# A decoder block on one core: the first token tile takes its norm weight per channel on the transposed rows, its loads go out on two queues, and constant products stand ahead of the first ones

## The chip, the core and the metric

The kernel runs on one core of one Trainium2 chip. TensorE (PE) multiplies; VectorE (DVE), ScalarE (ACT) and GpSimd (POOL) do the rest; SyncE (SP) issues most transfers from memory. The metric is the device time of one execution in microseconds (us). The kernel before took 1122.25 us (median of three runs, 1120.26 to 1123.79).

## The reference

One layer of a hybrid block over 512 tokens of width 1024, in float32:

```python
u = rmsnorm(h, norm_mix_pre_w[layer])          # x * rsqrt(mean(x*x) + eps) * w
proj = u @ w_in[layer]
q, k, v, z, xbc, dt_raw, gate_logits = jnp.split(proj, offsets, axis=-1)
# dilated attention on q, k, v; a Mamba-2 mixer on z, xbc, dt_raw; both projected,
# mixed by sigmoid gates, projected again, normed and added to h; then a squared-ReLU MLP
```

Only the first line and the `v` and `dt_raw` columns of the second one are touched here. The norm weight `w` has one value per channel.

## The kernel before

Every float32 product is made of three products of rounded halves: a matrix is split into a high part (`wh`, `uh`: a rounding copy on ACT) and a low part (`wl`, `ul`: the remainder, by a subtraction on DVE or POOL), and `three` issues high by high, low by high and high by low. Weights come as units of 1 MB through a two-deep pool (`ws` staging, `wh`, `wl`).

The start, from L264 on, makes `u` transposed (channels on partitions) for four tiles of 128 tokens. For a tile `i`, `square_u` squares the rows with a running sum (ACT, L300 and L303), adds eps (DVE, L301 and L304) and takes the power -1/2 on POOL (L305). `norm_u` (L309) multiplies the rows by this factor and by `row0`, the norm weight broadcast to all partitions. `transpose_u` (L212) turns eight blocks of 128 by 128 on PE into two PSUM banks `ut`. `split_u` (L321 and L322) makes `uh` and `ul` of a bank at a time, four channel blocks in one instruction.

Between these steps stand the splits of the first weight chunk, `split_v1` (L326, L327), in four pieces of two channel blocks. The three value chunks are then computed in the order 1, 0, 2 (`V_ORDER`), for four token tiles each, with the squares, norms and transposes of the tiles 1 to 3 put between the products of the tile before (`V_STEPS`). A product chunk is called `psv` in rows, chunk 1's being the first four. Chunk 0 also holds the `dt_raw` columns; its weights are `wh0` and `wl0` (L331, L332, the second half of `wl0` on POOL). The weights of chunk 2 come through the pool (L108) and are split by L90 and L93.

Two things set the order on an engine. Instructions marked with `pin` keep the order in which they are written; others are put by the scheduler. Not pinned are the splits of chunk 2, the exponential of `a_log` on ACT (L409, `rows`), and the evacuations `vtok`. Each engine then runs its list in order. Transfers on SP each take one of eight completion semaphores in turn, and a transfer waits until the one eight places before it has landed.

In the rows, `wh_v` and `wl_v` name the parts of any value chunk; the line tells which (L326 and L327 are chunk 1, L331 and L332 chunk 0, L90 and L93 chunk 2).

Of the kernel before, what the change touches and what calls it, by code (L numbers as in the profile page):

```python
# [11 lines left out]
F32 = mybir.dt.float32  # L12
# [6 lines left out]
P = 128  # L19
# [23 lines left out]
SSM_FILL = (2, 7, 4, 3, 9, 5, 6)  # L43
SSM_LAST = (3, 8, 4, 3, 9, 8, 8)

V_ORDER = tuple((d, i) for d in (1, 0, 2) for i in range(NT))
# [31 lines left out]
def hybrid_block(ctx: ExitStack, tc: tile.TileContext, a: dict):  # L78
# [126 lines left out]
    def pin(ins):  # L205
        return tc.keep_in_program_order(ins)
# [53 lines left out]
    with tc.tile_pool(name="start", bufs=1, reuse_waits="tile") as st:  # L260
# [9 lines left out]
        def load_x(i):  # L270
            for cs in (slice(0, T), slice(T, D)) if i == 0 else (slice(0, D),):
                sp.dma_start(xt[:, i, cs], a["x"][0, i * P : (i + 1) * P, cs])

        def load_row(cs):
            sp.dma_start(row0[:, cs], a["norm_mix_pre_w"][:, cs].broadcast_to([P, T]))
# [3 lines left out]
                         for n, dt in (("ws", F32), ("wh", F32R), ("wl", F32R))]  # L279
        load_row(slice(0, T))  # L280
        for k in range(0, KD, 2):
            sp.dma_start(v3(ws1, KD)[:, k : k + 2, :], w_in[:, k : k + 2, OFF_V + UC : OFF_V + 2 * UC])
            if k == 0:
                load_row(slice(T, D))
            if k == KD - 2:
                load_x(1)
        for i in range(2, NT):
# [8 lines left out]
        def square_u(i):  # L296
            un = uns[i] = st.tile([P, D], F32, name=f"un{i}", tag="un", bufs=2)
            if i == 0:
                for n, cs in enumerate((slice(0, T), slice(T, D))):
                    pin(act.activation(un[:, cs], xt[:, i, cs], AF.Square, scale=RD, accum_out=sq0[:, n : n + 1]))  # L300
                pin(dve.tensor_scalar(rs[:, i : i + 1], sq0[:, 0:1], sq0[:, 1:2], EPS, ALU.add, ALU.add))  # L301
            else:
                pin(act.activation(un, xt[:, i, :], AF.Square, scale=RD, accum_out=ssq[:, i : i + 1]))  # L303
                pin(dve.tensor_scalar(rs[:, i : i + 1], ssq[:, i : i + 1], EPS, None, ALU.add))  # L304
            pin(pool.tensor_tensor(rs[:, i : i + 1], rs[:, i : i + 1], mhalf, op=ALU.pow))  # L305

        def norm_u(i):
            for cs in (slice(0, T), slice(T, D)):
                pin(dve.scalar_tensor_tensor(uns[i][:, cs], xt[:, i, cs], rs[:, i : i + 1], row0[:, cs],  # L309
                                             op0=ALU.mult, op1=ALU.mult))  # L310
# [7 lines left out]
        def split_u(i, b):  # L318
            p3 = pts.pop((i, b)).rearrange("p (k t) -> p k t", k=4)
            hi = uh[:, 4 * b : 4 * b + 4, i * P : (i + 1) * P]  # L320
            pin(act.activation(hi, p3, AF.Copy))  # L321
            pin(dve.tensor_tensor(ul[:, 4 * b : 4 * b + 4, i * P : (i + 1) * P], p3, hi.bitcast(F32), op=ALU.subtract))  # L322

        def split_v1(k, eng=dve):
            ks = slice(k * UC, (k + 2) * UC)
            pin(act.activation(wh1[:, ks], ws1[:, ks], AF.Copy))  # L326
            pin(eng.tensor_tensor(wl1[:, ks], ws1[:, ks], wh1[:, ks].bitcast(F32), op=ALU.subtract))  # L327

        def split_v0(k, eng=dve):
            ks = slice(k, k + 4)  # L330
            pin(act.activation(wh0[:, ks, :], ws0[:, ks, :], AF.Copy))  # L331
            pin(eng.tensor_tensor(wl0[:, ks, :], ws0[:, ks, :], wh0[:, ks, :].bitcast(F32), op=ALU.subtract))  # L332

        square_u(0)
        norm_u(0)
        split_v1(0)
        transpose_u(0, 0)
        transpose_u(0, 1)
        split_v1(2, pool)
        split_u(0, 0)  # L340
        split_v1(4)
        split_u(0, 1)
        split_v1(6)
# [743 lines left out]
```

## Time and profile before

| | |
|---|---|
| median of 3 runs | 1122.25 us |
| the profiled execution | 1122.04 us, span 1120.3 us |
| PE busy in the span | 1094.8 us (98%) |
| DVE, ACT, POOL busy | 670.7, 482.2, 63.4 us |
| chain that ended last | PE 89%, DVE 7%, DMA 2% |
| TensorE's mean granted clock | 0.997 of full |

The span runs from the first to the last instruction of the execution; 1.7 us of the profiled execution lie around it. The page says that a busy PE is not PE at its peak, since matmul ends are modelled: the distance between the starts of two neighbours tells more than a duration. What the change touches lies in the first 45 us.

### The profile page before, as it was taken

The numbers are of one execution on the slowest core, as the hardware profiler recorded it, in microseconds if no ns is written. First come the engines' busy times: TensorE is split into PE (matmuls) and PEld (weight loads), VectorE is DVE, ScalarE is ACT, GpSimd is POOL, SyncE is SP. The second block draws the span as 40 slices with busy tenths as digits, with TensorE's granted clock in tenths as the row PEclk, the third lists the DMA queues.
The fourth block names the chain that finished last, engine by engine and source line by source line (L and its number), as shares of the span: only waits on it lengthen the run. The fifth ranks groups of instructions, "written<-read, shape, count | busy, mean of one in ns | idle before, by whom it ended". The sixth has DMA issues, their size and how long they took to land.

```text
span 1120.3 us, 13600 instructions
## 1 busy us (share of the span) xinstructions
PE 1094.8 (98%) x5501; PEld 909.5 (81%) x5501; DVE 670.7 (60%) x986; ACT 482.2 (43%) x803; POOL 63.4 (6%) x71
## 2 busy tenths in 40 slices
PE   6999999999999999999999999999999999999997
PEld 6988877778888787878787878889888888888886
DVE  5657665347786869696969685855433234333324
ACT  6256665463556363637272623443322233232321
POOL 2203222000000000000000000000000000000000
PEclk9999999999999999999999999999999999999999
DMA  8232212332333232332323222450332324223212
GB/s 274 77 114 77 69 45 66 104 94 77 112 97 129 76 113 80 108 100 89 113 75 113 76 76 77 187 188 1 113 113 75 113 86 159 102 86 114 75 38 75
DMA packets 86463, 110.86 MB, mean 99 GB/s; under 512 B 4080, under 2 KB 74224, under 8 KB 85376
## 3 DMA queue, kind: packets, MB, share of 16 engines
q1 hardware_dynamic: 85072, 101.01, 28.2%
q0 software_dynamic: 1328, 8.98, 2.1%
q8 instruction: 43, 0.70, 0.3%
q14 instruction: 20, 0.16, 0.0%
HBM read 107.81 MB, written 2.16 MB: 98 GB/s over the span
## 4 chain that ended last, share of the span: by engine, by line
PE 89%; DVE 7%; DMA 2%; issue 1%; ACT 1%; SPq 0%; POOL 0%; POOLq 0%; DVEq 0%; ACTq 0%
PE psu L209 16%; PE psd L209 15%; PE psx L209 8%; PE psbc L209 8%; PE psz L209 8%; PE pssp L209 5%; PE psga L209 4%; PE psgs L209 4%; PE psq L209 3%; PE psk L209 3%; PE psap L209 3%; PE psv L209 3%; PE pq L209 1%; PE po L209 1%; PE pt L212 1%; DVE acc L679 1%
## 5 line engine op out<-in xcount | busy, mean ns | idle before, releaser
L209 PE MATMUL psu<-fh,wh_up 128*128 128x512 f32 (+1 forms) x288 | 105.4, 366 | 0.0
L209 PE MATMUL psu<-fl,wh_up 128*128 128x512 f32 (+1 forms) x288 | 105.2, 365 | 0.0
L209 PE MATMUL psu<-fh,wl_up 128*128 128x512 f32 (+1 forms) x288 | 105.2, 365 | 0.0
L209 PE MATMUL psd<-wl_dn,hh 128*128 128x512 f32 x240 | 93.4, 389 | 0.0
L209 PE MATMUL psd<-wh_dn,hl 128*128 128x512 f32 x240 | 93.4, 389 | 0.0
L209 PE MATMUL psd<-wh_dn,hh 128*128 128x512 f32 x240 | 93.4, 389 | 0.0
L93 DVE TENSOR_TENSOR wl_up<-ws_up,wh_up 128x2048 fp32r<-128x2048 f32 x16 | 36.7, 2292 | 77.6 <-ACT wh_up L90 77.5
L93 DVE TENSOR_TENSOR hl<-hidden,hh 128x512 fp32r<-128x512 f32 x32 | 21.9, 693 | 77.3 <-ACT hh L90 77.2
L90 ACT ACTIVATE hh<-hidden 128x512 fp32r<-128x512 f32 x32 | 20.2, 632 | 103.1 <-PE psd L209 97.6
L209 PEld LDWEIGHTS psu<-fh,wh_up 128*128 128x128 f32 x288 | 54.3, 189 | 8.8
L209 PEld LDWEIGHTS psu<-fh,wl_up 128*128 128x128 f32 x288 | 54.3, 189 | 8.7
L209 PEld LDWEIGHTS psu<-fl,wh_up 128*128 128x128 f32 x288 | 54.3, 189 | 8.7
L90 ACT ACTIVATE wh_up<-ws_up 128x2048 fp32r<-128x2048 f32 x16 | 30.7, 1916 | 61.4 <-PE psu L209 56.1
L209 PEld LDWEIGHTS psd<-wh_dn,hh 128*128 128x128 f32 x240 | 45.0, 188 | 9.5
L209 PEld LDWEIGHTS psd<-wh_dn,hl 128*128 128x128 f32 x240 | 45.0, 188 | 9.4
L209 PEld LDWEIGHTS psd<-wl_dn,hh 128*128 128x128 f32 x240 | 45.0, 188 | 9.3
L209 PE MATMUL psx<-uh,wh_x 128*128 128x512 f32 x128 | 52.4, 410 | 0.0
L209 PE MATMUL psz<-uh,wh_z 128*128 128x512 f32 x128 | 51.1, 399 | 0.0
L209 PE MATMUL pssp<-yth,wh_sp 128*128 128x512 f32 x128 | 51.0, 399 | 0.0
L209 PE MATMUL psbc<-uh,wh_bc 128*128 128x512 f32 x128 | 50.8, 397 | 0.0
L209 PE MATMUL psz<-uh,wl_z 128*128 128x512 f32 x128 | 50.1, 392 | 0.0
L209 PE MATMUL pssp<-yth,wl_sp 128*128 128x512 f32 x128 | 50.1, 392 | 0.0
(271 smaller groups left out, 2792.4 us busy)
## 6 DMA issues: line engine op xcount, KB each, us to landing
ws_up<-in_w_up_dram SPq DMA_DIRECT2D x16, 1024.0 KB, 5.4
ws_dn<-in_w_down_dram SPq DMA_DIRECT2D x15, 1024.0 KB, 5.0
ws_z<-in_w_in_dram SPq DMA_DIRECT2D x8, 1024.0 KB, 5.2
ws_x<-in_w_in_dram SPq DMA_DIRECT2D x8, 1024.0 KB, 5.2
w<-acs_d POOLq DMA_DIRECT2D x8, 1024.0 KB, 5.0
ws_bc<-in_w_in_dram SPq DMA_DIRECT2D x16, 512.0 KB, 4.7
ws_sp<-in_w_ssm_proj_dram SPq DMA_DIRECT2D x8, 1024.0 KB, 4.8
ws_ga<-in_w_in_dram SPq DMA_DIRECT2D x4, 1024.0 KB, 5.3
```

What stands on the lines that cost most here:

```text
L90: ins = act.activation(hi, src, AF.Copy)
L93: (eng or dve).tensor_tensor(lo, src, hi.bitcast(F32), op=ALU.subtract)
L209: tc.keep_in_program_order(pe.matmul(*args, **kw))
L212: tc.keep_in_program_order(pe.transpose(dst, src, ident))
L679: dve.tensor_tensor(acc[o], acc[o], ps, op=ALU.add)
```

## The change

The first token tile is no longer multiplied by the broadcast norm weight. Its rows are only scaled by their own factor; after the transposes channels lie on partitions, and `split_u0` applies the weight as a scale per partition (`ncol`, 8 values per partition) in the same instructions that split, now one channel block at a time: eight on ACT and eight on DVE in place of two and two. The second half of the tile's rows is squared on DVE, by an instruction that multiplies and sums, beside the first half's square on ACT. That second half and `ncol` are loaded from ACT's queue. SP issues the four weight pieces and tile 1's rows before the two halves of `row0`. Eleven products of a constant tile stand at the head of PE's list, into a bank that nothing reads. The third piece of `wl` of chunk 1 moves from POOL to DVE.

```diff
         def load_x(i):
-            for cs in (slice(0, T), slice(T, D)) if i == 0 else (slice(0, D),):
-                sp.dma_start(xt[:, i, cs], a["x"][0, i * P : (i + 1) * P, cs])
+            if i == 0:
+                act.dma_start(xt[:, 0, T:], a["x"][0, 0:P, T:])
+                sp.dma_start(xt[:, 0, :T], a["x"][0, 0:P, :T])
+            else:
+                sp.dma_start(xt[:, i, :], a["x"][0, i * P : (i + 1) * P, :])
...
-        load_row(slice(0, T))
+
+        ncol = st.tile([P, KD], F32, name="ncol")
+        act.dma_start(ncol, a["norm_mix_pre_c"])
         for k in range(0, KD, 2):
             sp.dma_start(v3(ws1, KD)[:, k : k + 2, :], w_in[:, k : k + 2, OFF_V + UC : OFF_V + 2 * UC])
-            if k == 0:
-                load_row(slice(T, D))
-            if k == KD - 2:
-                load_x(1)
+        load_x(1)
+        load_row(slice(0, T))
+        load_row(slice(T, D))
...
-                for n, cs in enumerate((slice(0, T), slice(T, D))):
-                    pin(act.activation(un[:, cs], xt[:, i, cs], AF.Square, scale=RD, accum_out=sq0[:, n : n + 1]))
+                pin(act.activation(un[:, :T], xt[:, i, :T], AF.Square, scale=RD, accum_out=sq0[:, 0:1]))
+                pin(dve.tensor_tensor_reduce(un[:, T:], xt[:, i, T:], xt[:, i, T:], 1.0 / D, 0.0, ALU.mult, ALU.add,
+                                             sq0[:, 1:2]))
...
+                if i == 0:
+                    pin(dve.tensor_scalar(uns[i][:, cs], xt[:, i, cs], rs[:, i : i + 1], None, ALU.mult))
+                    continue
...
+        def split_u0(k):
+            pk = pts[0, k // 4][:, (k % 4) * P : (k % 4 + 1) * P]
+            hi = uh[:, k, 0:P]
+            pin(act.activation(hi, pk, AF.Copy, scale=ncol[:, k : k + 1]))
+            pin(dve.scalar_tensor_tensor(ul[:, k, 0:P], pk, ncol[:, k : k + 1], hi.bitcast(F32), op0=ALU.mult,
+                                         op1=ALU.subtract))
...
+        warm = gbank("warm")
+        for n in range(WARM):
+            mm(warm[:, 0:P], ones, ones, start=True, stop=True)
         square_u(0)
         norm_u(0)
-        split_v1(0)
         transpose_u(0, 0)
         transpose_u(0, 1)
-        split_v1(2, pool)
-        split_u(0, 0)
+        split_u0(0)
+        split_u0(1)
+        split_v1(0)
+        split_u0(2)
+        split_u0(3)
+        split_v1(2)
+        split_u0(4)
+        split_u0(5)
         split_v1(4)
-        split_u(0, 1)
+        split_u0(6)
+        split_u0(7)
         split_v1(6)
         square_u(1)
```

The scheduler's order differs only in the first 45 us. On ACT, the work of the first tile (`uh` out of `ut`, the pieces `wh_v` of chunk 1) stood so before:

```order
L326 ACTIVATE wh_v_108<-ws_v_107 128x512 [waits DMAHW3_49]
L326 ACTIVATE wh_v_108<-ws_v_107 128x512 [waits DMAHW5_49]
L321 ACTIVATE uh<-ut_0_133 128x4x128 [waits PE_49]
L326 ACTIVATE wh_v_108<-ws_v_107 128x512 [waits DMAHW6_49]
L321 ACTIVATE uh<-ut_1_138 128x4x128 [waits PE_49]
L326 ACTIVATE wh_v_108<-ws_v_107 128x512 [waits DMAHW7_49]
```

And now, the first half of the same list (semaphores in brackets; DMAHW ones are a transfer's landing):

```order
L337 ACTIVATE uh<-ut_0_145,ncol 128x128 [waits DMAHW2_49,PE_49]
L337 ACTIVATE uh<-ut_0_145,ncol 128x128 [waits DVE_49]
L343 ACTIVATE wh_v_108<-ws_v_107 128x512 [waits DMAHW3_49]
L337 ACTIVATE uh<-ut_0_145,ncol 128x128 [waits DVE_49] x2
L343 ACTIVATE wh_v_108<-ws_v_107 128x512 [waits DMAHW4_49]
```

Each `uh` but the first of a bank now waits for DVE's `ul` of the block before it.

Further on in ACT's list, the tiles 1 to 3 stood so before (`un` are squares, `rows` the exponential of `a_log`, `vtok` evacuations; `wh_v_101` is chunk 0, `wh_v_314` chunk 2):

```order
L303 ACTIVATE un_187,ssq<-xt 128x1024
L321 ACTIVATE uh<-ut_0_200 128x4x128
L321 ACTIVATE uh<-ut_1_205 128x4x128
L365 ACTIVATE vtok<-psv_0_177 128x256
L303 ACTIVATE un_230,ssq<-xt 128x1024
L321 ACTIVATE uh<-ut_0_240 128x4x128
L409 ACTIVATE rows<-rows 128x32
L321 ACTIVATE uh<-ut_1_245 128x4x128
L365 ACTIVATE vtok<-psv_1_223 128x256
L321 ACTIVATE uh<-ut_0_282 128x4x128
L321 ACTIVATE uh<-ut_1_287 128x4x128
L331 ACTIVATE wh_v_101<-ws_v_100 128x1152 x2
```

And now (`wh_v_340` is chunk 2):

```order
L310 ACTIVATE un_213,ssq<-xt 128x1024
L436 ACTIVATE rows<-rows 128x32
L331 ACTIVATE uh<-ut_0_226 128x4x128
L331 ACTIVATE uh<-ut_1_231 128x4x128
L392 ACTIVATE vtok<-psv_0_203 128x256
L310 ACTIVATE un_256,ssq<-xt 128x1024
L331 ACTIVATE uh<-ut_0_266 128x4x128
L331 ACTIVATE uh<-ut_1_271 128x4x128
L392 ACTIVATE vtok<-psv_1_249 128x256
L92 ACTIVATE wh_v_340<-ws_v_338 128x1024 x2
L331 ACTIVATE uh<-ut_0_308 128x4x128
L331 ACTIVATE uh<-ut_1_313 128x4x128
```

The exponential moved from the middle of tile 2 to ahead of tile 1's split, and chunk 2's high parts from behind chunk 0's to ahead of tile 3's split.

On DVE, the end of the same stretch stood so before (`ul` from `ut_0_282` on is tile 3, `wl_v_102` chunk 0, `wl_v_315` chunk 2):

```order
L309 SCALAR_TENSOR_TENSOR un_230<-xt,rs,row_98 128x512 x2
L322 TENSOR_TENSOR ul<-ut_0_282,uh 128x4x128
L322 TENSOR_TENSOR ul<-ut_1_287,uh 128x4x128
L332 TENSOR_TENSOR wl_v_102<-ws_v_100,wh_v_101 128x1152
L93 TENSOR_TENSOR wl_v_315<-ws_v_312,wh_v_314 128x1024 x2
```

And now:

```order
L319 SCALAR_TENSOR_TENSOR un_256<-xt,rs,row_98 128x512 x2
L95 TENSOR_TENSOR wl_v_341<-ws_v_338,wh_v_340 128x1024 x2
L332 TENSOR_TENSOR ul<-ut_0_308,uh 128x4x128
L332 TENSOR_TENSOR ul<-ut_1_313,uh 128x4x128
L349 TENSOR_TENSOR wl_v_102<-ws_v_100,wh_v_101 128x1152
```

Chunk 2's low parts moved ahead of tile 3's. On POOL, the power for tile 3 moved behind three small multiplications of `cw`, `cb` and `bg`.

## Rows read from the trace of the kernel before

**Rows 1.** Busy time by stretch; PE busy, PEld, DVE, ACT, POOL, PEclk, DMA share, GB/s.
```profile
19.90:52.00 32.10, 32.10 (x260) 32.10 (x259) 20.75 (x39) 11.59 (x21) 10.09 (x8) 1.00 0.45 139
...
200.00:790.00 590.00, 580.23 (x3013) 480.92 (x3012) 429.36 (x626) 281.52 (x480) 17.28 (x24) 1.00 0.31 99
```
**Rows 2.** The chain of waits from 0 to 60 us: start, length, what.
```profile
4.79 7.55 DMA xt<-in_x_dram
...
12.36 1.16 ACT un L303 x2
...
23.70 28.63 PE psv L209 x228
```
**Rows 3.** PE in order of time: start, duration, instruction, idle time before and its releaser.
```profile
7.76 1.12 PE L212 MATMUL ut<-ident,un 128*128 128x128 f32 x4 [7.76 <-DVE un L309]
...
12.51 0.41 PE L209 MATMUL psv<-wh_v,uh 128*128 128x256 f32 x1
12.72 0.41 PE L209 MATMUL psv<-wl_v,uh 128*128 128x256 f32 x1
...
14.27 0.28 PE L209 MATMUL psv<-wl_v,uh 128*128 128x256 f32 x1
14.39 0.28 PE L209 MATMUL psv<-wh_v,ul 128*128 128x256 f32 x1
...
24.98 0.29 PE L209 MATMUL psv<-wh_v,uh 128*128 128x256 f32 x1
```
**Rows 4.** The waits of PE from 200 us on: total, times, longest.
```profile
PE pyo L209 <- DVE prev L759: 9.6, 11, 1.4
```
**Rows 5.** ACT in order of time, same columns as PE's.
```profile
9.59 0.63 ACT L326 ACTIVATE wh_v<-ws_v 128x512 fp32r<-128x512 f32 x1 [1.38 <-DMA ws_v<-in_w_in_dram]
10.13 0.58 ACT L321 ACTIVATE uh<-ut 128x512 fp32r<-128x512 f32 x1
...
15.94 1.19 ACT L321 ACTIVATE uh<-ut 128x512 fp32r<-128x512 f32 x2 [1.08 <-PE ut L212]
...
19.76 0.22 ACT L409 ACTIVATE rows<-rows 128x32 f32<-128x32 f32 x1
...
26.65 2.01 ACT L90 ACTIVATE wh_v<-ws_v 128x1024 fp32r<-128x1024 f32 x2
```
**Rows 6.** DVE in order of time.
```profile
6.96 0.75 DVE L309 SCALAR_TENSOR_TENSOR un<-xt,rs,row 128x512 f32<-128x512 f32 x1 [1.82 <-DMA row<-in_norm_mix_pre_w_dram]
...
14.37 1.41 DVE L309 SCALAR_TENSOR_TENSOR un<-xt,rs,row 128x512 f32<-128x512 f32 x2 [0.67 <-POOL rs L305]
```
**Rows 7.** SP's queue in order of time: start and duration of an issue.
```profile
0.73 0.84 SPq L272 DMA_DIRECT2D xt<-in_x_dram  x2
...
11.27 3.67 SPq L346 DMA_DIRECT2D rows<-in_dt_bias_dram  x1
14.98 0.43 SPq L346 DMA_DIRECT2D rows<-in_a_log_dram  x1
...
20.12 0.38 SPq L108 DMA_DIRECT2D ws_v<-in_w_in_dram  x1
```
**Rows 8.** Transfers issued from 11 to 24 us: size, us from issue to landing.
```profile
ws_v<-in_w_in_dram SPq DMA_DIRECT2D x1, 1024.0 KB, 5.4
...
rows<-in_a_log_dram SPq DMA_DIRECT2D x1, 16.0 KB, 4.4
```
**Rows 9.** Groups by shape on ACT, 0 to 60 us: busy, mean ns, idle before.
```profile
L397 ACT ACTIVATE dt<-dt 128x128 f32<-128x128 f32 x1 | 0.3, 310 | 0.8 <-DVE dt L396 0.8
```
**Rows 10.** Groups by shape on DVE, 0 to 60 us.
```profile
L322 DVE TENSOR_TENSOR ul<-ut,uh 128x512 fp32r<-128x512 f32 x8 | 5.3, 687 | 3.1 <-ACT uh L321 3.1
...
L93 DVE TENSOR_TENSOR wl_q<-ws_q,wh_q 128x1024 fp32r<-128x1024 f32 x2 | 2.3, 1210 | 0.0
L327 DVE TENSOR_TENSOR wl_v<-ws_v,wh_v 128x512 fp32r<-128x512 f32 x3 | 2.1, 711 | 0.0
L404 DVE SCALAR_TENSOR_TENSOR dt<-dt,dt 128x128 f32<-128x128 f32 x7 | 2.0, 292 | 0.2
```

More of the change, by code (lines that the diff above doesn't have):

```diff
@@ L44 @@
 SSM_LAST = (3, 8, 4, 3, 9, 8, 8)
+WARM = 11
 V_ORDER = tuple((d, i) for d in (1, 0, 2) for i in range(NT))
@@ L1072 @@
     data["ssm_norm_w"] = data["ssm_norm_w"][0].reshape(16, P).T
+    data["norm_mix_pre_c"] = data["norm_mix_pre_w"][0].reshape(8, P).T
     data["d_skip"] = _np.repeat(data["d_skip"][0], P // 2).reshape(16, P).T
```

## The prediction

> **What bounds the kernel now.** I read the busy times by stretch first. From 19.9 us to 52 PE is busy all the time, and between 200 and 790 us 580.2 of 590 us [rows 1]; what PE loses at the start is therefore not made up by waiting for something else just after. The chain of waits says the same of the start: up to 12.36 us it waits for the rows of tile 1 to land, goes through their square and norm, and from 23.70 us it is 28.63 us of products without a break [rows 2]. So the question is when PE gets through the last piece of chunk 1, tile 3, whose first product starts at 24.98 us and whose third, the first to read `ul`, comes some 0.24 us later, at 25.22 (the products at 14.27 and 14.39 are 0.12 apart) [rows 3]. Everything behind it keeps its order on every engine, so I take its shift as the kernel's shift.
>
> Then I read ACT and DVE in order of time, since the change alters their lists. ACT runs its list strictly: at 9.59 us it had been idle 1.38 us for a weight piece, and the rounding of the first transposed bank, whose operand PE began at 7.76, had to stand behind it until 10.13 [rows 3, 5]. An instruction that waits for a landing holds all that is listed after it. That decides this change.
>
> **The first tile, earlier.** Before, DVE could start the norm at 6.96 us only because it waited 1.82 us for the broadcast weight [rows 6]; that wait goes, and one of two squares leaves ACT, for some 0.6 us more (the gap between two 128x512 copies there is 0.54 [rows 5]; the form on DVE isn't in the trace: at the cheapest 128x512 form, 0.69, it ends with ACT's square, at twice that the gain is gone). So the norm starts at about 4.6 to 5.2 us, and the transposes at 6.0, having 7.76 before. I cost the eleven constant products at nothing: PE is idle there until 7.76 [rows 3]. Should the transposes have to wait for them, a microsecond is lost in a place that, as follows, no longer decides.
>
> **The first tile, then slower.** Per pair of channel blocks the new lists alternate: `uh` on ACT (0.31), `ul` on DVE (0.29), the next `uh`, which waits for that `ul` (0.31), a weight piece's high part (0.63), its low part on DVE (0.71), and only then the next pair's `ul`, since DVE's list has it behind the low part. In steady state a pair costs the second `uh`, the high part, the low part and the first `ul` of the next pair: 0.31 + 0.63 + 0.71 + 0.29 = 1.94 us [rows 5, 9, 10]. (The 128x128 forms read SBUF there, PSUM here; above, each is bounded by the 0.69 of a whole bank.) If ACT alone decided it would be 2 x 0.31 + 0.63 = 1.25. Four pairs from about 6.7 us on: 14.5 us, or 11.7 at best. ACT's square of tile 1 follows, 1.06 and 0.19 of read-out, then eps, power and norm: before, that took from 12.36 to 14.37 [rows 2, 6], so the norm of tile 1 starts at 16.5 (13.7 at best) against 14.37. The early start is spent.
>
> **The wait for `a_log`.** The exponential now stands ahead of tile 1's `uh`. Its operand was issued at 14.98 us and took 4.4 [rows 7, 8]: 19.4. Before, it ran at 19.76, after tile 1's `uh` of 15.94 [rows 5], and cost nothing. Now tile 1's `uh` cannot start before 19.4 + 0.22 = 19.6. Behind it in ACT's list stand tile 1's second half, an evacuation and the square of tile 3; DVE's `ul`, the norm of tile 2 (behind `ul` in its list) and so tile 2's transposes wait for it. From `uh` to the end of tile 2's products I count: 0.58 + 0.69 until `ul`, 0.69 for the second `ul`, the norm of tile 2 (1.41), four transposes (0.5), half a group of products (1.4), a whole one (2.9) with eight transposes (1.0): 9.2 us, so that tile 3's first product could start at 28.8. That alone is 3.8 us late.
>
> **The wait for chunk 2's weights.** Both ACT and DVE now split chunk 2 ahead of tile 3. These weights were issued at 20.12 us and took 5.4 [rows 7, 8]: 25.5. Then the first high half takes 1.06 (26.6; two took 2.01 [rows 5]), the two low halves 1.21 each [rows 10] (29.0), tile 3's first `ul` 0.69 (29.7). Before, the product that reads it started at 25.22: 4.4 us late. The two waits run beside each other and don't add: the later one, this one, counts. Chunk 0 follows with no further loss: its POOL half ends 2.8 us after its high part, as before, and tile 3's products and half a group of chunk 0 cover it (2.6 + 1.6 us).
>
> **When these transfers land now.** SP's list from the third tile's rows on is the same, and so are the bytes ahead. The 3.67 us issue of `dt_bias` [rows 7] shows that the queue was full then, and the issues behind it came as it drained. The front is relieved by one issue of 0.42 us, now on ACT. I take 0.5 us earlier: 25.0, and tile 3 then 3.9 us late. Bounds: not earlier at all (4.4), or 1.9 earlier, if half of the 3.67 us goes (2.5); if all of it went, chunk 2 would make 0.7 us, but then tile 1 is held by its own norm, 16.5 against 14.37, 2.1 us.
>
> The second queue is the place where the Trainium skill speaks against the change. "DMA: Bandwidth & Descriptors", section "Issuing engines are not separate DMA queues", says that transfers started by different engines share the same 16 DMA engines and that only the issuer's time is saved. By that the halves land 0.4 us earlier at most, as I took above; were the second queue worth both issues of the first rows, 0.84 us [rows 7], tile 3 would be 3.6 us late. No row here has two queues at once.
>
> **The sum.** Gains: none reaches tile 3. Loss: 3.9 us, with a little for a TensorE that is idle or sparsely used until 19 us: before, its 128x256 products were 0.21 us apart at 12.51 and 12.72 and 0.12 at 14.27 and 14.39 [rows 3], which is 1.2 and 2.4 GHz, though the granted clock reads 1.00 for the stretch after [rows 1]. If it stands at the lower level when tile 1 is released, 24 products cost 24 x 0.09 = 2.2 us and eight transposes about 1, of which 0.9 is hidden behind the chunk 2 wait: up to 2.3 more. I allow 0.1 as the likeliest, since the later products catch up. 4.0 us on the profiled execution, 1122.04 (1120.3 span and 1.7 around it, which stays): 1126.0. The median lies 0.2 higher; on it I forecast 1126.2 us. Own range of this case: 2.5 to 6.7 us, 1124.7 to 1129.0.
>
> **Rivals.**
>
> *Something later takes the delay up.* PE waits 9.6 us from 200 us on, eleven times for DVE's states [rows 4]. If DVE came to these at times that don't depend on the start, 4 us of delay would vanish in them: 1122 to 1123. For it: DVE is busy 429 of 590 us there [rows 1]. Against: what DVE works on comes from PE's products of the same group, and PE is busy all the way from the start to the first group. With it I count the case that the transfers land 1.1 us or more earlier, tile 3 then 2.1 to 3.3 us late: some 1125.0. Together 0.24.
>
> *The start's gain reaches the end.* If the four pairs run at ACT's 1.25 us, tile 1's norm starts at 13.7 instead of 14.37, and PE gets 0.7 us; if the 18 products ahead of tile 1's transposes (three for each of six channel blocks) run 0.12 apart and not 0.21, 18 x 0.09 = 1.6 us more are saved on them. 1122.25 - 2.3 = 1120.0, faster. It decides only where `a_log` lands by 14.5 and chunk 2's weights by 20.5, five microseconds earlier than in the trace. "TensorE: Matmul & The Clock Gate", section "Part 1: The HAM clock gate", of the Trainium skill says that the clock is throttled by default and that activity releases it; by that the constant products do what they are put there for. The trace agrees: with PE at work, the distance fell between 12.72 and 14.27 us [rows 3]. A faster clock does nothing against a wait for an operand. 0.08.
>
> *TensorE at its lower level for the whole of tile 1 and 2,* and POOL's half of chunk 0 late by a microsecond as well: 7 us or more, 1129.3 and above. 0.06.
>
> The forecast has the rest, 0.62. That the change doesn't do what it says I don't count apart: the lists show it done.
>
> **How the numbers follow.** About 0.3%, 3.4 us, is what a measurement of this kernel can tell from no change. Of the forecast's 0.62 some 0.06 lies under it (landings half a microsecond earlier still), of the first rival all but 0.01, of the second 0.03. Slower: 0.56 + 0.01 + 0.06 = 0.63; faster 0.05; within 0.32. The range leaves out the last rival's upper part and the faster one: 1121.8 to 1129.2.
>
> **What would show it.** Right: ACT idle before the exponential until about 19 us, for two microseconds or more, with tile 1's `uh` right behind it; ACT idle before chunk 2's high part until about 25, tile 3's `uh` behind it; tile 3's first `psv` product near 29; everything after it shifted by the same time. The first tile's pairs 1.9 us apart. Wrong: a landing of `a_log` before 16 us, or of chunk 2's weights before 22; a tile 3 on time; or a first group of the state-space part that starts 4 us late with PE's waits from 200 us on shorter by as much.

## The result, and the profile after

The changed kernel takes 1126.29 us (median of 9 runs, one of which took 2869 us and is no part of the ratio) against 1122.04 us for the kernel before (median of 9): a ratio of 1.0037, 95% interval 1.0026 to 1.0049, which is 4.2 us on the median. 1126.2 us was forecast. The profiled execution of after took 1127.02 us, 4.98 us more than that of before, with a span of 1125.2 us (1120.3 before).

The PE rows show where this stands in the program (columns as in [rows 3]). First three more of before, then those of after:

```profile
15.27 1.23 PE L212 MATMUL ut<-ident,un 128*128 128x128 f32 x8 [0.60 <-DVE un L309]
...
18.61 1.34 PE L212 MATMUL ut<-ident,un 128*128 128x128 f32 x8
...
27.86 0.30 PE L209 MATMUL psv<-wh_v,uh 128*128 128x288 f32 x1
```

```profile
6.91 1.09 PE L214 MATMUL ut<-ident,un 128*128 128x128 f32 x8 [0.69 <-DVE un L317]
...
17.78 1.94 PE L214 MATMUL ut<-ident,un 128*128 128x128 f32 x8 [2.48 <-DVE un L319]
...
23.36 1.22 PE L214 MATMUL ut<-ident,un 128*128 128x128 f32 x8
...
30.43 0.39 PE L211 MATMUL psv<-wh_v,ul 128*128 128x256 f32 x1 [0.44 <-DVE ul L332]
...
33.16 0.30 PE L211 MATMUL psv<-wh_v,uh 128*128 128x288 f32 x1
```

The first tile's transposes start at 6.91 us (7.76 before), but those of tile 1 at 17.78 (15.27). The third product of tile 3, the forecast's mark, comes at 30.43 us, 5.21 after the 25.22 worked out in the prediction. The last row is the first product of chunk 0, the first of the 288-wide form, which stood at 27.86 before: 5.30 late. I use that product as the mark from here on.

The mark's delay stays to the end (the span is 4.9 us longer). From 200 to 790 us PE is busy 580.22 of 590 us, as before [rows 1], and its waits there have the same size [rows 4]. First the row by stretch, then that of the waits:

```profile
200.00:790.00 590.00, 580.22 (x3015) 480.47 (x3012) 428.50 (x626) 279.09 (x478) 17.24 (x24) 1.00 0.31 99
```

```profile
PE pyo L211 <- DVE prev L786: 9.7, 11, 1.4
```

The chain of waits of after, from 0 to 60 us, against [rows 2]:

```profile
14.99 1.04 ACT un L310 x2
...
16.88 0.76 DVE un L319
...
17.78 1.94 PE ut L214 x8
19.72 3.84 PE psv L211 x18
...
27.42 1.97 DVE wl_v L95 x2
...
29.68 0.70 DVE ul L332
...
30.43 27.23 PE psv L211 x214
```

Three things are late in it. ACT's square of tile 1 starts at 14.89 us (the chain counts it from 14.99), where before it started at 12.36. Then PE itself is on the chain for 3.84 us, with 18 products. Then chunk 2's low part stands ahead of tile 3's `ul`. The landing of `a_log` is not on the chain at all.

ACT's rows (columns as in [rows 5]) show the pairs and the two waits of the forecast.

```profile
8.39 0.37 ACT L337 ACTIVATE uh<-ut,ncol 128x128 fp32r<-128x128 f32 x1 [0.42 <-DVE ul L338]
...
10.29 0.37 ACT L337 ACTIVATE uh<-ut,ncol 128x128 fp32r<-128x128 f32 x1 [0.75 <-DVE ul L338]
...
14.89 1.04 ACT L310 ACTIVATE un<-xt 128x1024 f32<-128x1024 f32 x1
...
18.59 0.23 ACT L436 ACTIVATE rows<-rows 128x32 f32<-128x32 f32 x1 [1.53 <-DMA rows<-in_a_log_dram]
18.91 0.60 ACT L331 ACTIVATE uh<-ut 128x512 fp32r<-128x512 f32 x1
...
26.32 2.00 ACT L92 ACTIVATE wh_v<-ws_v 128x1024 fp32r<-128x1024 f32 x2
28.22 1.08 ACT L331 ACTIVATE uh<-ut 128x512 fp32r<-128x512 f32 x2
```

From 8.39 to 10.29 is one pair: 1.90 us. The exponential waits for `a_log` and tile 1's `uh` stands right behind it, as forecast. Chunk 2's high part stands ahead of tile 3's `uh`, also as forecast, but it shows no wait for a landing: the weights had come. DVE's rows, against [rows 6], complete this.

```profile
6.37 0.88 DVE L317 TENSOR_SCALAR un<-xt,rs 128x512 f32<-128x512 f32 x2 [0.74 <-POOL rs L312]
...
16.88 1.42 DVE L319 SCALAR_TENSOR_TENSOR un<-xt,rs,row 128x512 f32<-128x512 f32 x2 [0.67 <-POOL rs L312]
...
29.68 1.28 DVE L332 TENSOR_TENSOR ul<-ut,uh 128x512 fp32r<-128x512 f32 x2
```

What the forecast hardly had is in the busy times by stretch (columns as in [rows 1]; the figure behind POOL's is the granted clock).

```profile
5.00:10.00 5.00, 2.70 (x15) 1.97 (x14) 2.79 (x9) 1.64 (x6) 0.55 (x1) 1.00 0.95 311
10.00:15.00 5.00, 4.65 (x17) 4.00 (x17) 3.22 (x8) 3.19 (x9) 0.00 (x0) 0.51 1.04 387
15.00:20.00 5.00, 2.52 (x13) 2.25 (x13) 2.79 (x6) 3.13 (x7) 1.10 (x2) 0.50 0.81 221
20.00:25.00 5.00, 5.00 (x30) 5.00 (x30) 2.58 (x6) 2.60 (x6) 2.02 (x4) 0.63 0.95 288
```

TensorE stands at its lower level, 1.2 of 2.4 GHz, from about 10 to 23 us. In tile 1 that shows as eight transposes in 1.94 us (1.23 before, at 15.27) and values products 0.21 us apart instead of 0.12. From the start of tile 1's transposes to that of tile 2's takes 5.58 us (17.78 to 23.36) against 3.34 before (15.27 to 18.61).

SP's queue and the transfers, against [rows 7] and [rows 8]:

```profile
10.57 3.44 SPq L373 DMA_DIRECT2D rows<-in_dt_bias_dram  x1
14.06 0.43 SPq L373 DMA_DIRECT2D rows<-in_a_log_dram  x1
...
19.23 0.38 SPq L110 DMA_DIRECT2D ws_v<-in_w_in_dram  x1
```

```profile
ws_v<-in_w_in_dram SPq DMA_DIRECT2D x1, 1024.0 KB, 5.7
...
rows<-in_a_log_dram SPq DMA_DIRECT2D x1, 16.0 KB, 4.5
```

`a_log` lands at 18.6 us (18.9 forecast) and chunk 2's weights at 24.9 (25.0 forecast).

So the 5.30 us fall into three pieces, read as differences of times: tile 1's transposes 2.51 late (17.78 against 15.27), the way from there to tile 2's transposes 2.24 longer (5.58 against 3.34), and the rest, 0.55, behind them, with chunk 2's low part ahead of tile 3's `ul`. The experiments have to show that these are what they look like.

### The profile page after: what moved, and what is told of

The parts are those of the page before. It is cut to its first block, busy times and chain, and to the rows that moved or that the text cites. A ratio compares the mean times of both kernels' runs of the same rounds, so it can differ in the third digit from the quotient of the medians.

```text
span 1125.2 us, 13656 instructions
## 1 busy us (share of the span) xinstructions
PE 1102.5 (98%) x5523; PEld 917.1 (81%) x5523; DVE 671.6 (60%) x995; ACT 482.7 (43%) x807; POOL 62.3 (6%) x70
## 4 chain that ended last, share of the span: by engine, by line
PE 88%; DVE 7%; ACT 1%; DMA 1%; issue 1%; POOL 0%; POOLq 0%; DVEq 0%; ACTq 0%
PE psu L211 16%; PE psd L211 15%; PE psx L211 8%; PE psbc L211 8%; PE psz L211 8%; PE pssp L211 5%; PE psga L211 4%; PE psgs L211 4%; PE psk L211 3%; PE psq L211 3%; PE psap L211 3%; PE psv L211 3%; PE pq L211 1%; PE po L211 1%; PE pt L214 1%; DVE acc L706 1%
## 5 line engine op out<-in xcount | busy, mean ns | idle before, releaser
L211 PE MATMUL pssp<-ytl,wh_sp 128*128 128x512 f32 x128 | 50.2, 392 | 0.0
```

Source lines behind the costliest of these rows:

```text
L211: tc.keep_in_program_order(pe.matmul(*args, **kw))
```

## The experiments

Theory T says: the first tile's alternating 128x128 pairs make tile 1 late by itself; the lower clock after the constant products adds as much; and the two waits for landings that the forecast counted hide behind these. Rival W says that one of the two waits sets the time, as the forecast had it, and the other two are idle time off the path. Each kernel below the first row ran in five rounds against the kernel before. The table gives the mark (chunk 0's first product in the profiled execution; 27.86 before) and the time.

| kernel | mark, us | against before | median, us | ratio, 95% interval |
|---|---|---|---|---|
| changed kernel | 33.16 | +5.30 | 1126.29 | 1.0037, 1.0026 to 1.0049 |
| exponential behind | 32.49 | +4.63 | 1126.56 | 1.0042, 1.0028 to 1.0056 |
| both behind | 32.16 | +4.30 | 1125.08 | 1.0031, 1.0019 to 1.0043 |
| kept warm | 34.00 | +6.14 | 1127.09 | 1.0049, 1.0037 to 1.0062 |
| both behind, kept warm | 30.28 | +2.42 | 1124.54 | 1.0022, 1.0012 to 1.0031 |
| banks in turn | 30.39 | +2.53 | 1122.73 | 1.0015, 1.0006 to 1.0024 |
| banks in turn, both behind | 27.82 | -0.04 | 1120.83 | 0.9994, 0.9985 to 1.0003 |
| the same, kept warm | 28.40 | +0.54 | 1121.95 | 0.9997, 0.9987 to 1.0006 |
| before + constant products | 27.69 | -0.17 | 1121.51 | 0.9995, 0.9986 to 1.0004 |
| before + second queue | 26.89 | -0.97 | 1120.04 | 0.9987, 0.9978 to 0.9995 |
| bank scaled | 27.37 | -0.49 | 1121.19 | 0.9996, 0.9987 to 1.0005 |
| bank scaled, kept warm | 27.39 | -0.47 | 1119.67 | 0.9986, 0.9977 to 0.9995 |
| the same, DVE for POOL | 26.34 | -1.52 | 1119.88 | 0.9980, 0.9972 to 0.9989 |

Read the mark for the size of a term and the ratio for the verdict. Ratio times 1121.5 us gives shifts that agree with the mark's within 1.2 us, 0.6 under it in the mean; each ratio has an interval of about 1 us either way, and the mark comes from one execution.

**Both behind.** The exponential and chunk 2's splits are held behind the values, where they stood before.

```diff
-                    split(stage[:, f], hi[:, f], lo[:, f], eng, pinned=key == "o1")
+                    split(stage[:, f], hi[:, f], lo[:, f], eng, pinned=key in ("o1", "v2"))
...
-        act.activation(rows[:, 1, :], rows[:, 1, :], AF.Exp)
+        pin(act.activation(rows[:, 1, :], rows[:, 1, :], AF.Exp))
```

Expected: 

> Edit: the changed kernel with the two moved waits put back: the exponential of a_log and chunk 2's splits are pinned behind tile 3's split, as they stood before the change. Theory W (the prediction's: the waits for a_log and for chunk 2's weights are what is late, each worth about 3.8 us or more by itself): the loss goes, 1122 to 1123 us, tile 3's first product that reads ul near 26. Theory T (the first tile's alternation makes tile 1 late by itself, and TensorE at 1.2 GHz adds to it; the waits hide behind that): only PE's stall ahead of tile 3's ul goes, 0.6 us at most: 1125.7, that product at 29.8 instead of 30.43.

Measured: 1.0031 (1.0019 to 1.0043), the mark 1.00 us earlier. W's 1122 to 1123 us is refuted; the two waits together are worth less than a microsecond at the mark as the kernel stands: of the 1.00, 0.17 was there already when tile 1's transposes started (17.61 against 17.78), which the edit doesn't touch.

**The exponential behind, alone.** Only the edit of the exponential.

```diff
-        act.activation(rows[:, 1, :], rows[:, 1, :], AF.Exp)
+        pin(act.activation(rows[:, 1, :], rows[:, 1, :], AF.Exp))
```

Expected: 

> The changed kernel with the exponential of a_log alone held behind the values; chunk 2's splits stay ahead of tile 3's. Theory T (a_log's wait was hidden: TensorE's transposes of tile 1 come after the landing anyway): chunk 0's first product stays within 0.3 us of the changed kernel's 33.16, and the time at 1126.0 us (ratio 1.0034 to 1.0041). Rival (the prediction's own step: a_log alone makes tile 1 up to 3.8 us late): chunk 0's first product at 30.5 or earlier, and the time under 1124.5 us (ratio under 1.0028).

Measured: 1.0042 (1.0028 to 1.0056). ACT's row for tile 1 (columns as above) gives the reason:

```profile
18.85 0.60 ACT L331 ACTIVATE uh<-ut 128x512 fp32r<-128x512 f32 x1 [1.84 <-PE ut L214]
```

Without the exponential in front, tile 1's `uh` starts at 18.85 instead of 18.91: it waits for PE's transposes. So the wait for `a_log` cost 0.06 us at most, and next to nothing counted from the start of these transposes (1.12 us here, 1.13 there). The mark moved by 0.67, more than T's 0.3; the granted clock reads 0.71 here and 0.51 in the changed kernel from 10 to 15 us, 0.77 and 0.63 from 20 to 25, so in that execution the clock fell later and rose earlier. No run shows whether the edit had a part in that.

**Kept warm.** Constant products between the first tile's pairs (`keep_warm(m)` issues m of them): 5 behind its transposes, 4 behind its second and its fourth step, 12 ahead of tile 1's transposes.

```diff
+        keep_warm(5)
         split_u0(0)
...
+                if (d, i) == (1, 0) and k in (1, 3, 5):
+                    keep_warm(12 if k == 5 else 4)
```

Expected: 

> Edit: the changed kernel with further constant products (5 behind tile 0's transposes, 4 behind the channel blocks 1 and 3 of the first group, 12 behind block 5), where PE is idle otherwise. Theory T: the clock stays at 2.4 GHz, the products of tile 1 stand 0.12 apart instead of 0.21, and tile 3's first product that reads ul comes 1.3 us earlier, at 29.1 (then chunk 2's split, put ahead of it, holds it): 1125.0. Theory W: no change in time, since the waits decide: 1126.3.

Measured: 1.0049 (1.0037 to 1.0062), no gain; T's time was missed. The clock reads 1.00 in every stretch to 30 us, and tile 2's last product started 2.45 us earlier than in the changed kernel (27.02 against 29.47). Then ACT, and PE behind it:

```profile
25.67 2.01 ACT L92 ACTIVATE wh_v<-ws_v 128x1024 fp32r<-128x1024 f32 x2 [1.69 <-DMA ws_v<-in_w_in_dram]
```

```profile
28.21 0.39 PE L211 MATMUL psv<-wh_v,uh 128*128 128x256 f32 x1 [0.91 <-ACT uh L331]
...
29.78 0.39 PE L211 MATMUL psv<-wh_v,ul 128*128 128x256 f32 x1 [1.06 <-DVE ul L332]
...
30.33 0.41 PE L211 MATMUL psv<-wh_v,ul 128*128 128x256 f32 x1
30.55 0.41 PE L211 MATMUL psv<-wh_v,uh 128*128 128x256 f32 x1
```

This is the wait that the forecast counted: ACT idle for chunk 2's weights, tile 3's third product at 29.78. It is real, and the late first tile had covered it. Right behind PE's waits of 0.91 and 1.06 us the clock fell again (products 0.22 us apart at 30.33), and what was left of the gain was lost: 0.65 us at the third product became 0.84 late at the mark.

**Both behind, and kept warm.** The two edits together.

Expected: 

> The changed kernel with both edits of the first two experiments: the exponential of a_log and chunk 2's splits held behind, and constant products between the first tile's pairs. Theory T (the first tile's lateness, the lower clock after it, and the two waits ahead of tile 1's and tile 3's splits each hide behind the other): with the waits gone the clock's part shows, tile 1's transposes take 1.2 us instead of 1.9, values products are 0.12 us apart, tile 3's third product comes at about 27.1 and chunk 0's first at 30.0, 2.2 us before the kernel with the exponential alone held behind; the time is 1123.2 us (1122.6 to 1123.8). Rival W (the lower clock costs nothing on the way to tile 3, since something else is late there): chunk 0's first product stays near 32.1 and the time near 1125.1 us.

Measured: 1.0022 (1.0012 to 1.0031), the mark at 30.28 as T had it (30.0), and the granted clock 1.00 in every stretch. The time is 1.3 us over T's 1123.2; the ratio, 2.5 us, fits the mark's 2.42. The transposes of tile 1:

```profile
17.77 1.23 PE L214 MATMUL ut<-ident,un 128*128 128x128 f32 x8 [0.38 <-DVE un L319]
```

They start at 17.77, as in the changed kernel, and take 1.23 us; those of tile 2 start at 21.10, 3.33 later, as before. So with the waits gone the clock is worth 32.16 - 30.28 = 1.9 us at the mark, and what remains, 2.4, is the first tile itself. The times alone don't show the clock's part: the interval overlaps that of the version without the products (1.0019 to 1.0043).

**Banks in turn.** The first tile takes its channels from the two transposed banks alternately (0, 4, 1, 5, ...) with the same instructions.

```diff
-        split_u0(0)
-        split_u0(1)
-        split_v1(0)
...
+        for j in range(4):
+            split_u0(j)
+            split_u0(4 + j)
+            split_v1(2 * j)
```

Expected: 

> Edit: the changed kernel with the first tile's channel blocks split in the order 0, 4, 1, 5, 2, 6, 3, 7, so that ACT and DVE work on different PSUM banks. Both theories: a round falls from 1.91 to about 1.2 us, and ACT squares tile 1 three microseconds earlier, at 12. Theory T with the waits behind it: tile 1's uh then waits for a_log until 18.9 as now, and little is gained, 0.5 to 1.1 us: 1125.5. Theory T without any weight of the waits: the whole 3 us are gained: 1123.3.

Measured: 1.0015 (1.0006 to 1.0024), the mark 2.77 us earlier, so nearer to the forecast without the waits. A round of two splits and a weight piece now takes 1.1 us instead of 1.9:

```profile
9.98 0.62 ACT L337 ACTIVATE uh<-ut,ncol 128x128 fp32r<-128x128 f32 x2
...
11.10 0.63 ACT L337 ACTIVATE uh<-ut,ncol 128x128 fp32r<-128x128 f32 x2
```

The scheduler also moved chunk 2's splits behind chunk 0's here, and one `uh` ahead of the exponential, so this is no single edit. The run uncovers the other wait, in ACT's rows:

```profile
15.70 0.60 ACT L331 ACTIVATE uh<-ut 128x512 fp32r<-128x512 f32 x1 [1.38 <-PE ut L214]
18.99 0.23 ACT L428 ACTIVATE rows<-rows 128x32 f32<-128x32 f32 x1 [2.69 <-DMA rows<-in_a_log_dram]
19.12 0.58 ACT L331 ACTIVATE uh<-ut 128x512 fp32r<-128x512 f32 x1
```

With tile 1 early, `a_log` does hold its second half, for 2.7 us.

**Banks in turn, both behind.** Both edits.

Expected: 

> Edit: the two edits together, the waits put back behind and the banks in turn. If the late first tile and the waits hide each other, as theory T has it, the gains of the two single edits (0.6 and about 0.8) don't add to this one: 4 to 5 us, 1121.8, level with the kernel before. If each had its own share, it is the sum of the single gains.

Measured: 0.9994 (0.9985 to 1.0003), the mark where it was before. The pairs' order and the two waits account for the whole loss, the clock's part with them (with tile 1 early the clock is back by 15 us). And they don't add: alone, the edits bring the mark 1.00 and 2.77 us forward, together 5.34, since each uncovers what the other removes.

**The same, kept warm,** with POOL's products of `cw`, `cb` and `bg` behind the fourth tile's norm.

```diff
+        keep_warm(5)
         for j in range(4):
...
-            pool.tensor_scalar(t, t, 0.5, None, ALU.mult)
+            pin(pool.tensor_scalar(t, t, 0.5, None, ALU.mult))
```

Expected: 

> The changed kernel with the first tile's channels taken from the two transposed banks in turn, the exponential and chunk 2's splits held behind, and besides constant products between the first tile's pairs, and POOL's products of cw, cb and bg behind the power of the fourth tile's norm. Theory T: against the version without these last two (1120.8 us) the clock is 1.00 from 10 to 15 us too and the 0.5 us wait for rs is gone: chunk 0's first product at 26.9 to 27.4 (27.82 there), 1120.1 us (1119.6 to 1120.6). Rival (the clock's part there is hidden by the wait for the norm of tile 1, and the next landing takes the place of rs): 1120.8 us.

Measured: 0.9997 (0.9987 to 1.0006), no gain. The clock now fell in the wait for tile 1's norm:

```profile
14.90 1.94 PE L214 MATMUL ut<-ident,un 128*128 128x128 f32 x8 [1.70 <-DVE un L319]
```

The products ahead of that wait were done sooner (the last starts at 12.92), the wait was 1.70 us in place of 1.36, and the transposes ran at the lower level, 1.94 us. Here a faster clock ahead of a wait made the wait longer.

**Before, with the constant products alone.**

```diff
+        warm = gbank("warm")
+        for n in range(WARM):
+            mm(warm[:, 0:P], ones, ones, start=True, stop=True)
         square_u(0)
```

Expected: 

> The kernel before with the 11 constant products alone put ahead of its first transposes. Theory T (the constant products themselves cost nothing: TensorE has nothing else to do before the first tile's transposes, and the clock of before is full in every stretch anyway): 1121.5 us, no change (1121.2 to 1121.8), tile 3's third product still at about 25.2. Rival (the constant products bring the granted clock down again later, in the first tile's sparse products): granted clock under 0.8 between 10 and 20 us, the transposes of tile 1 at twice their time, and 0.5 to 1.5 us more, 1122.0 to 1123.0 us.

Measured: 0.9995 (0.9986 to 1.0004), no change, as T had it, though the clock does in part what the rival said. By stretch:

```profile
10.00:15.00 5.00, 5.00 (x22) 4.27 (x20) 3.67 (x8) 4.36 (x9) 1.83 (x2) 0.50 1.04 385
15.00:20.00 5.00, 4.90 (x39) 4.41 (x39) 3.62 (x8) 3.51 (x8) 1.10 (x2) 0.99 0.79 229
```

It costs nothing since before, too, the first tile's products were 0.21 us apart up to 13.6 us [rows 3], though the same stretch of before read 1.00:

```profile
10.00:15.00 5.00, 4.67 (x22) 3.93 (x21) 3.65 (x7) 4.53 (x9) 1.83 (x2) 1.00 1.04 391
```

In both, tile 1 came after the clock's rise: its transposes take 1.23 us in either. The constant products buy a fast clock for a stretch in which PE waits. No run here leaves the 11 products out of the changed kernel, so whether they or the sparse first tile brought its clock down is not shown.

**Before, with the second queue alone.**

```diff
-            for cs in (slice(0, T), slice(T, D)) if i == 0 else (slice(0, D),):
-                sp.dma_start(xt[:, i, cs], a["x"][0, i * P : (i + 1) * P, cs])
+            if i == 0:
+                act.dma_start(xt[:, 0, T:], a["x"][0, 0:P, T:])
+                sp.dma_start(xt[:, 0, :T], a["x"][0, 0:P, :T])
```

Expected: 

> The kernel before with the second half of the first token tile alone loaded from ScalarE's queue (all else as before, the norm weight's rows still loaded first). Theory T (a start 0.3 to 0.7 us earlier does not reach the end, because the first norm waits for the row of the norm weight and the weights' landings set tile 3): 1121.3 us (1120.9 to 1121.6). Rival (the start bounds the first 25 us): the gain of the earlier half, 0.5 us or more, is seen at chunk 0's first product (27.3 or less against 27.86) and at the end, 1120.9 us or less.

Measured: 0.9987 (0.9978 to 0.9995). T falls, the rival holds: a microsecond reaches the mark and the end. The chain of waits names it:

```profile
4.37 7.01 DMA xt<-in_x_dram
...
11.40 1.16 ACT un L306 x2
```

Tile 1's rows are issued 0.42 us earlier than in [rows 2], by the one issue that left SP, and take 7.01 instead of 7.55: they land 0.97 earlier (in the run with the constant products alone, without any edit of a transfer, 0.18), and their square was the first thing of that chain that waited. The Trainium skill, "DMA: Bandwidth & Descriptors", section "Issuing engines are not separate DMA queues", says that a second issuer saves only the time it takes to initiate. The 0.42 fits that; the other 0.54 is in the transfer's own time, and no run here shows why.

**Bank scaled.** To beat both: the transposed rows are multiplied by the weight a bank at a time, so the first tile has 128x512 splits again. The two waits are held behind here too, and tile 1's square stands ahead of chunk 1's last low part, which goes to POOL.

```diff
+            pin(dve.tensor_tensor(us[:, bs, :], p3, ncol[:, bs].unsqueeze(2).broadcast_to([P, 4, P]), op=ALU.mult))
...
+            pin(act.activation(uh[:, bs, 0:P], us[:, bs, :], AF.Copy))
+            pin(dve.tensor_tensor(ul[:, bs, 0:P], us[:, bs, :], uh[:, bs, 0:P].bitcast(F32), op=ALU.subtract))
...
         square_u(1)
+        split_v1(6, pool)
```

Expected: 

> A version meant to beat both: as the changed kernel, but the first tile's transposed rows are scaled a bank at a time (one VectorE product of 128x512 with the weights' column repeated over the tokens, written over the first tile's x, then one 128x512 split each on ScalarE and VectorE in place of eight 128x128 pairs), tile 1's squares ahead of the last of chunk 1's splits, whose low part goes to POOL, and the exponential, chunk 2's splits and POOL's products of cw, cb and bg held behind. Theory T (the 128x128 pairs were what ate the earlier start): tile 1's norm at 12.6 us (16.88 in the changed kernel), its transposes at 13.4, chunk 0's first product at 26.0, 1.8 us before the kernel before, and 1119.6 us (1119.0 to 1120.4). Rival (tile 1 then waits for its x or its row of the norm weight, or tile 0's products at the lower clock end after 13.4): chunk 0's first product at 27 to 28 and 1120.8 us, no better than the kernel with the banks in turn.

Measured: 0.9996 (0.9987 to 1.0005), the mark at 27.37, 1.4 us behind T and inside the rival's 27 to 28, but for another reason. The norm of tile 1 started at 12.88, near T's 12.6, but took 2.42 us.

**Bank scaled, kept warm,** with 14 constant products.

```diff
+        keep_warm(5)
         scale_u0(0)
...
+                if (d, i) == (1, 0) and k in (1, 3, 5):
+                    keep_warm(5 if k == 5 else 2)
```

Expected: 

> The version that scales a bank at a time, with 14 more constant products in the first tile (5 after its transposes, 2 behind its second and its fourth step, 5 ahead of tile 1's transposes). Theory T: if the version without them shows a granted clock under 0.9 between 10 and 20 us, this one is 0.5 to 1 us faster than it (1118.9 us), with tile 1's transposes in 1.2 us; if its clock is full there, no change. Rival (the constant products stand ahead of tile 1's transposes and hold them): 0.5 us slower than it.

Measured: 0.9986 (0.9977 to 0.9995), while the mark did not move (27.39), though the granted clock from 10 to 15 us rose from 0.66 to 1.00: the norm still decides when tile 1 starts. Whether the ratio's gain over the version without them is a real one, the overlapping intervals leave open.

**The same, DVE for POOL.** Chunk 1's last low part goes behind the norm on VectorE, and 2 constant products stand ahead of tile 1's transposes instead of 5. The edit is against the kernel just above.

```diff
         square_u(1)
-        split_v1(6, pool)
+        norm_u(1)
+        split_v1(6)
...
-                    keep_warm(5 if k == 5 else 2)
+                    keep_warm(2)
```

Expected: 

> The version that scales a bank at a time with constant products, with the low part of the last split of chunk 1 on VectorE, behind tile 1's norm, in place of POOL beside it, and 2 constant products in place of 5 ahead of tile 1's transposes. There tile 1's two norm products took 2.42 us beside POOL's split (12.88 to 15.3), against 1.41 us in the kernel before. Theory C (VectorE's norm products and POOL's split of 128x512 get in each other's way): the norm takes 1.41 us again, tile 1's transposes start at 13.8 (14.81 there), chunk 0's first product comes at 26.4 (27.39 there), and the time is 1118.8 us, ratio 0.9972 to 0.9982. Rival (the norm's length came from the row of the norm weight still being written, or tile 2's x is the next bound): the norm stays over 2 us or chunk 0's first product over 27.1, and the time at 1119.7 us.

Measured: 0.9980 (0.9972 to 0.9989), faster than before and, by 6.4 us in the medians, than the changed kernel. The mark is at 26.34, where theory C had 26.4; its ratio came as well, its 1118.8 us was missed by 1.1 in the median. First DVE's and POOL's rows of the kernel with POOL, then DVE's of this one:

```profile
12.90 2.42 DVE L319 SCALAR_TENSOR_TENSOR un<-xt,rs,row 128x512 f32<-128x512 f32 x2 [0.67 <-POOL rs L312]
```

```profile
12.84 1.28 POOL L349 TENSOR_TENSOR wl_v<-ws_v,wh_v 128x512 fp32r<-128x512 f32 x1
```

```profile
12.85 1.42 DVE L319 SCALAR_TENSOR_TENSOR un<-xt,rs,row 128x512 f32<-128x512 f32 x2 [0.67 <-POOL rs L312]
```

The norm starts at the same time and takes 1.42 us when POOL is idle beside it. The Trainium skill, "GPSIMD Engine Reference", section "1. Specifications", says that POOL shares its interfaces to the memory with VectorE and contends with VectorE instructions that read two operands from there. The norm does (`xt` and `row`), and the pair of rows agrees: 1.00 us.

## Why the prediction was right, and where only its sum was right

The time was right on the median (1126.2 forecast, 1126.29 measured), and so was the place: the start, up to tile 3, with nothing given back later. At its own mark the sum was short: tile 3's third product was forecast 3.9 us late and came 5.21 late, and the profiled execution was to be 4.0 us longer and was 4.98. The sum was made of one term, the wait for chunk 2's weights, and the delay was mostly made of others; that the two totals are so near is in part luck. One sign of being right that the prediction named did not come: ACT was to idle before chunk 2's high part until about 25 us, and it shows no wait there. The idle time before the exponential was 1.53 us, where two or more were named. The terms follow one by one; the first rests on ACT's first square, before and after:

```profile
3.52 0.63 ACT L300 ACTIVATE un<-xt 128x512 f32<-128x512 f32 x1 [1.52 <-DMA xt<-in_x_dram]
```

```profile
4.40 0.63 ACT L305 ACTIVATE un<-xt 128x512 f32<-128x512 f32 x1 [1.48 <-DMA xt<-in_x_dram]
```

- *The first tile, earlier.* The transposes were forecast at 6.0 us and came at 6.91. Of the 1.82 us that DVE idled before, the first part held POOL's power (5.29 to 5.84 us) and not only the wait for the weight. And the rows landed later, not earlier: ACT's square of the first half starts at 4.40 instead of 3.52, DVE's of the second at 4.60, the norm at 6.37. It decided nothing of the verdict, but moved the pairs 0.9 us on.
- *The first tile, then slower.* Right: 1.94 us a pair forecast, 1.90 measured; tile 1's norm at 16.5 forecast, 16.88 measured (the pairs started 0.9 us later than forecast and took 0.5 less in all). The low part that moved to DVE is the second of the four (`split_v1(2, pool)`), not the third. This is the largest term, 2.4 us with all else removed, and the forecast had it only as the floor under the two waits (2.1 us).
- *The wait for `a_log`.* The landing was right (18.9 and 18.6 us), the price wrong: "That alone is 3.8 us late." It was set against tile 1's `uh` of before and not against the late one: with the norm at 16.5 and the 1.57 us from norm to `uh` of before, `uh` could not start before 18.1 anyway. Measured alone: 0.06 us at most. Behind an early tile 1 it does hold it, 2.69 us.
- *The wait for chunk 2's weights.* Right in place, order and landing (25.0 and 24.9), and, where nothing hides it, in size: with the clock kept up tile 3's third product came at 29.78, and the forecast said 29.1 to 29.7 (29.7 is 4.5 us behind 25.22, where the prediction wrote 4.4). In the changed kernel tile 2 was nearly as late on PE, and the wait left about 0.5 us of it.
- *The clock.* The term that was mis-sized: 0.1 us allowed, "up to 2.3 more" named and set aside "since the later products catch up"; 2.2 us measured between the two tiles' transposes (5.58 against 3.34: eight transposes 0.71 longer and 18 products further apart, not 24), 1.9 when it is taken away by itself. It did not add in full, since its time and the wait for chunk 2 run beside each other: with the clock up the wait holds tile 3's third product until 29.78, with the clock down it comes at 30.43.
- *The rivals.* Nothing later took the delay up: PE's waits from 200 us on are 9.7 us (9.6 before). The start's gain did not reach the end, but the run with the second queue alone shows that a gain at the start can: -0.13% (-0.22 to -0.05), where nothing makes the first tile slower.

So the number came out because terms that run side by side have about the size of the longest, and two of them, the late tile at a low clock and the wait for chunk 2, were nearly equally long: 30.4 us at tile 3's third product by the one, 29.8 by the other. At the mark, removing the two waits alone gained 1.0 us, holding the clock up alone nothing, the banks in turn 2.8; the banks in turn and the waits together gained 5.3.

## What to carry to other kernels

When several waits run beside each other, work out for each when its waiter could start without it in the changed order, not in the old one; and expect that removing one alone shows little. Splitting a 128x512 step into 128x128 steps that hand over between two engines cost the hand-over each time, here 1.9 us a pair where the banks in turn took 1.1. The fastest kernel here (0.9980) keeps 128x512 splits and pays for one wide extra product a bank; it holds other edits as well, and no run compares that product alone with the banks in turn. Constant products paid, 1.9 us at the mark, where they filled PE's waits up to the work that they warm; where a wait of 1.70 us was left in between, the clock fell in it.

## What the runs showed of the hardware that had not been expected

- In the changed kernel the granted clock fell at about 10 us, behind a stretch in which PE was busy 2.70 of 5 us, with waits of 0.69, 1.32 and 0.34 us; it stayed down from 10 to 15 us while PE was busy 4.65 of 5. In the kernel kept warm it fell right behind waits of 0.91 and 1.06 us, in "the same, kept warm" within one of 1.70. The Trainium skill, "TensorE: Matmul & The Clock Gate", section "Part 1: The HAM clock gate", ties the fall to an engine that has been idle; in these runs PE had idled in part of the time only.
- The granted clock reads 1.00 for the start of the kernel before, while products were 0.21 us apart [rows 3]; with constant products ahead the same stretch reads 0.50. Here the spacing is the better witness.
- Moving one 0.42 us issue to another queue brought a later landing forward by 0.97 us in the one execution profiled, while the first rows landed later: ACT's first square starts at 4.05 to 4.40 us in the twelve kernels with the second queue, at 3.52 and 3.79 in the two without.
- A 128x512 split on POOL beside two 128x512 norm products on DVE cost these 1.00 us. The kernel before pays such a price too: chunk 2's two low halves took 3.86 us from 27.75 on, partly beside POOL's half of chunk 0 (26.58 to 29.39 us), and 2.36 in the changed kernel with POOL idle beside them.
